# A routing table of 64-byte entries, three expert chunks loaded ahead of the rows, 17 chunk buffers and experts in program order

## The chip, the cores and the metric

The kernel runs on one core of a Trainium2 chip. The core has five engines that run their own instruction streams and wait for each other by semaphores: TensorE (PE; its weight loads are listed as PEld), VectorE (DVE), ScalarE (ACT), GpSimd (POOL) and SyncE (SP). Transfers are issued from the queues of SP, ACT and POOL and carried out by 16 DMA engines. The metric is the device time of one execution in microseconds; lower is better.

## The reference

Two transformer blocks follow each other on 512 tokens of 1024 features, all in float32. The first has sliding-window attention, a gated delta rule and an MLP; the second has retention and differential attention. All the edits lie in the mixture of experts that closes the second block:

```python
def hierarchical_moe(h, w_rg, b_rg, w_re, b_re, w1, w3, w2):
    gp = softmax(h @ w_rg + b_rg);  g_top, g_idx = top_k(gp, 1)        # 4 groups
    el = (h @ w_re + b_re).reshape(T, 4, 8) of the group g_idx
    e_val, e_idx = top_k(el, 2)                                        # 2 of 8 experts
    weights = g_top * softmax(e_val);  expert = g_idx * 8 + e_idx
    # each token goes through its two experts (of 32):
    y = sum over both of weights * ((silu(h @ w1[e]) * (h @ w3[e])) @ w2[e])
x = x + g2 * y
return rmsnorm(x, norm_final)
```

w1 and w3 are 1024 x 512 for each expert, w2 is 512 x 1024: 6 MB of weights per expert, 192 MB for all 32.

## The kernel before

After the projection `w_out` the kernel writes the block's rows to HBM (`x1_rows` stores x1d, `rows` stores the normalised h2d), routes the tokens (`route`, `tables`) and sorts the 1024 pairs of token and expert by expert. `weigh` stores a table `tab` (1024 entries of 8 bytes: token number and weight, in sorted order); `tables` makes the indices `ix` with which an expert's entries are found in it. `sorted_x` gathers the tokens' rows from h2d in sorted order, 128 at a time, with eight indirect DMAs on POOL's queue, transposes them on TensorE (tile pxs) and puts them into `xs`. Four of the eight rows lie in two chunk buffers (`spare`) that are lent for it.

Each expert is worked on in windows of the sorted pairs. The letters of `PLAN` say how many: H is half a window (64 pairs), F a full one (128), E one and a half, D two. The places in this list are filled at run time: an expert with more pairs comes to a larger place (`etab` holds which expert stands where, so chunk loads from place 3 on read their expert from `etab` into a register of SP). Places 0 to 2 are fixed.

The weights come in 1 MB chunks of 128 x 2048. An expert has six: 0 to 3 hold gate and up, 4 and 5 the down projection. They are loaded in one order, written out in `places`: four chunks of experts 0 and 1, their downs, and then for each expert j its chunks 0 and 1, the downs of j-1, and its chunks 2 and 3; last come the downs of expert 31. Before the change the chunks go in turn through 16 buffers: eight called eraw (pool r8, also used elsewhere) and eight spare. Chunks 0 to 7 are loaded during `w_out` (`ahead`); `fetch` issues six more after the last row store (`issue_after(self.rowed)`), two more behind the gathers, and `use` issues chunk n+16 where chunk n is used. The loads are issued on SP and wait there for their buffer.

In `experts`, `look` reads an expert's entries of `tab` by an indirect DMA on POOL's queue into a small tile `note` and doubles the token numbers for half windows on VectorE (L1929), since half windows write rows of 512. `up` computes gate and up into PSUM tiles ph (and pu), `gated` makes `es` from them (ACT and DVE), `turn` transposes it (paT, then ea on ACT), `down` multiplies with chunks 4 and 5 (py), scales by g2 on VectorE (ey) and scatters the result with an accumulating indirect DMA on POOL's queue, in turns to x1d and yd. Three notes are read ahead (`AHEAD`). A scheduler orders the instructions of each engine; in the expert loop TensorE's order too is the scheduler's choice.

The last two experts (`BIDE` = 30 and 31) aren't scattered: their results are added to the rows by one-hot matmuls (`closing`, `select`, `place`, tile pl). `gather` loads the rows of x1d and yd into tiles rowf (SP, L2048), POOL adds them (L2052), then come pl, the final norm and the store of `out`.

Of the kernel before, what the change touches and what calls it, by code (L numbers as in the profile page):

```python
# [9 lines left out]
F32 = mybir.dt.float32  # L10
# [7 lines left out]
P = 128  # L18
S = 512
# [7 lines left out]
NMORE = 8  # L27
# [24 lines left out]
PLAN = "HHHHHHHEHHHHHHHDHHHHHHHFHFHHHFHH"  # L52
# [227 lines left out]
class K:  # L280
# [1079 lines left out]
    def moe(self):  # L1360
        nc, tc, T = self.nc, self.tc, self.T
        with ExitStack() as es:
            mo = self.mo = es.enter_context(self.pool("mo"))
            with ExitStack() as sc:
                rp = sc.enter_context(self.pool("route", "right"))

                self.scraps = [[t, 0] for t in (self.cs, self.sn)]
                self.scraps += [[self.wp.tile([P, 1024], F32, name="scrap", tag=g, bufs=n), 0]
                                for g, n in (("wraw", 2), ("wraw", 2))]
                for g in ("c5", "c2"):  # L1370
                    self.ct[g] = self.scrap(rp, [_COFF[g][1]], g)
                    nc.sync.dma_start(self.ct[g], T[g])
                self.router_end(rp)
                self.x1_rows(0)
                self.rows()
                self.x1_rows(1)
                with ExitStack() as self.late:
                    self.tables(rp, self.route(rp))
            self.right.close()
            with ExitStack() as rs:  # L1380
                self.extra = rs.enter_context(self.pool("extra"))
                self.rowp = rs.enter_context(self.pool("rowp", "right"))
                self.post = rs.enter_context(self.pool("post", "right"))
                self.xs = self.post.tile([P, KT, 9 * P], F32, name="xs")
                self.g2 = self.post.tile([P, D], F32, name="g2row")
                self.g2h = self.post.tile([P, 512], F32, name="g2half")
                self.use, fetch = self.places()
                rows = [self.spare() for _ in range(2)]
                with self.tc.issue_after(self.rowed):
                    fetch(6 + NMORE)  # L1390
                self.sorted_x(rows)
                fetch(8 + NMORE)
                for b in range(2):
                    pg = self.pt("pg2")
                    self.rowbc(pg, self.mod[:, 5 * KT + 4 * b:5 * KT + 4 * b + 4], 4)
                    nc.scalar.activation(self.g2[:, b * 512:(b + 1) * 512], pg, AF.Copy)
                    h = slice(b * HALF, (b + 1) * HALF)
                    nc.vector.tensor_copy(self.g2h[h], self.g2[h, b * 512:(b + 1) * 512])
                self.experts()

    def eload(self, src):
        raw = self.wide("eraw") if self.nraw % (8 + NMORE) < 8 else self.spare()
        self.nraw += 1
        last = self.nc.sync.dma_start(raw, src)
        self.loaded = getattr(last, "ins", last)
        return raw

    def spare(self):
        return self.extra.tile([P, 2048], F32, name="spare", bufs=NMORE)

# [72 lines left out]
    def route(self, ap):  # L1483
# [90 lines left out]
        def weigh():  # L1574
# [34 lines left out]
            nc.scalar.dma_start(self.tab.rearrange("(b p) c -> p b c", p=P), sw)  # L1609
# [26 lines left out]
    def tables(self, ap, then):  # L1636
# [55 lines left out]
        V.scalar_tensor_tensor(off, off, BIG, wrow, op0=ALU.mult, op1=ALU.add)  # L1692
        self.ix = self.mo.tile([P, NBLK * NE], I32, name="ix")
        V.tensor_add(self.ix.rearrange("p (b e) -> p b e", b=NBLK), win, off)
# [25 lines left out]
    def note(self, ix):  # L1720

        nc = self.nc
        t = self.post.tile([P, 2], I32, name="note", bufs=NE + len(SECOND))
        nc.gpsimd.memset(t, int(BIG))
        nc.gpsimd.indirect_dma_start(
            out=t, out_offset=None, in_=self.tab[:, :], in_offset=bass.IndirectOffsetOnAxis(ap=ix, axis=0),
            bounds_check=2 * S - 1, oob_is_err=False)
        return t
# [21 lines left out]
    def sorted_x(self, more):  # L1750

        nc = self.nc
        nc.vector.memset(self.xs[:, :, 2 * S:], 0.0)
# [3 lines left out]
        for b, row in enumerate(rows):  # L1757
# [5 lines left out]
            for h in range(2):  # L1763
# [8 lines left out]
                else:  # L1772
                    nc.vector.tensor_add(dst, src, self.sh2[:, k].unsqueeze(2).to_broadcast([P, 4, P]))
        self.gathered = last.ins
# [34 lines left out]
    def gated(self, pss, ws):  # L1809
        nc = self.nc  # L1810
        out = []
        with self.tc.high_priority(offset=HP):
            for (few, g, u, _), w in zip(pss, ws):
                s = self.post.tile([P, 512], F32, name="es", bufs=3)
# [7 lines left out]
    def turn(self, few, s):  # L1822
# [6 lines left out]
        a = self.post.tile([P, 4, P], F32, name="ea", bufs=3)[:, :, :m]  # L1829
# [4 lines left out]
    def down(self, aa, use, ixs, stay=False):  # L1834
# [47 lines left out]
    def places(self):  # L1882
# [19 lines left out]
        def fetch(n):  # L1902
            nonlocal pos
            while pos < min(n, len(order)):
                self.raws[order[pos]] = self.eload(source(*order[pos]))
                pos += 1
# [6 lines left out]

    def experts(self):
        nc, tc, T = self.nc, self.tc, self.T
        ET = mybir.EngineType
        notes, self.tok, self.idx = {}, {}, {}
        windows = lambda j: [(b * NE + j, m) for b, m in enumerate(WIN[j])]

        def look(j):  # L1920

            notes[j] = [], []
            for i, m in windows(j):
                t = self.note(self.ix[:, i:i + 1])
                ix = t[:, 0:1]
                if m == HALF:

                    i2 = self.post.tile([P, 1], I32, name="note2", bufs=NE)
                    nc.vector.tensor_scalar(i2, ix, 2.0, self.c("side"), op0=ALU.mult, op1=ALU.add)  # L1929
                    if j >= BIDE:  # L1930
                        self.idx[j] = i2
                        self.tok[j] = self.mo.tile([P, 1], F32, name=f"tok{j}")
                        nc.vector.tensor_copy(self.tok[j], ix)
                    ix = i2
                notes[j][0].append(t[:, 1:2].bitcast(F32))
                notes[j][1].append(ix)

# [12 lines left out]
        with tc.issue_after(behind):  # L1950
            for j in range(AHEAD):
                look(j)
        for j in range(NE):
            if j == 0:
                xs = [self.xs[:, :, 0:HALF]]
            else:
                xs = [self.window(self.load(self.wtab[0:1, i:i + 1], 2 * S, ET.Activation), m) for i, m in windows(j)]
            pss = self.up_begin(xs)
            last = j - 1 if j - 1 in held else None
            for c in range(4):  # L1960
                if c == 2 and last is not None and j != 1:
                    turn(last)
                    down(last)
                    behind = self.scattered
                self.up(pss, c, self.use(j, c))
            held[j] = self.gated(pss, notes[j][0])
            if j == 1:
                for i in range(2):
                    turn(i)
                    down(i)  # L1970
                behind = self.scattered
            if j + AHEAD < NE:
                with tc.issue_after(behind):
                    look(j + AHEAD)
# [137 lines left out]
```

## Time and profile before

| what | value |
|---|---|
| runs | 1924.11 us median of 3 (1922.74 to 1925.02) |
| profiled execution | 1929.74 us |
| its span in the trace | 1927.9 us |
| PE busy | 1836.7 us (95%) |
| DVE, ACT, POOL busy | 833.5, 622.2, 305.7 us |
| bytes moved | 359.63 MB, mean 187 GB/s |
| granted TensorE clock, mean | 0.979 |

The span is what the trace covers; the execution's own time is 1.84 us longer. A row of a time line reads: start, duration, engine, line, operation, out<-in, count, and in brackets how long the engine was idle before and what ended that. The mean load of the DMA engines is low over the whole span, because the first three quarters are matmuls on weights that are loaded along the way; the expert stage fills the last quarter.

### The profile page before, as it was taken

Reading aid. Unit: us, or ns where it says so; the run is one execution under the profiler, and the core shown is the slowest. Engines: PE = TensorE matmul, PEld = TensorE weight load, DVE = VectorE, ACT = ScalarE, POOL = GpSimd, SP = SyncE. Lnnn points to the kernel's source line nnn. Section 1 sums busy time; section 2 is a strip of 40 time slices with the busy share of each in tenths; the row PEclk is TensorE's granted clock in tenths of the full one; section 3 lists DMA queues with packets and bytes.
Section 4 is the critical chain, followed back from the end, with each engine's and each line's share of the span. In section 5 each row is a group of like instructions: output and inputs, shape, how many; then the busy total and the mean of one; then the engine's idle time right before and its main releaser. Section 6 shows DMA issues by size and latency. Waiting matters only on the chain.

```text
span 1927.9 us, 23285 instructions
## 1 busy us (share of the span) xinstructions
PE 1836.7 (95%) x8926; PEld 1315.3 (68%) x8926; DVE 833.5 (43%) x1561; ACT 622.2 (32%) x1031; POOL 305.7 (16%) x290
## 2 busy tenths in 40 slices
PE   8999999999999999999999999999879987999984
PEld 6888898788888888888777888888633322333322
DVE  6666656565565666654424343443411110110114
ACT  6454534433232344644442333322321110111102
POOL 0122122100000002421110000002212121121113
PEclk9999999899999999999999999999889999999998
DMA  5321004344554532222222222344779999999995
GB/s 184 88 66 39 6 23 142 90 156 164 186 186 159 194 114 91 80 71 73 77 60 89 92 82 80 120 164 169 271 282 404 417 402 414 381 395 417 404 419 209
DMA packets 76290, 359.63 MB, mean 187 GB/s; under 512 B 13034, under 2 KB 13546, under 8 KB 48528
## 3 DMA queue, kind: packets, MB, share of 16 engines
q1 hardware_dynamic: 63104, 321.55, 44.7%
q0 software_dynamic: 10304, 33.60, 5.6%
q10 hardware_dynamic: 2768, 2.96, 0.5%
q8 instruction: 71, 1.16, 0.2%
q14 instruction: 43, 0.35, 0.1%
HBM read 345.48 MB, written 18.36 MB: 189 GB/s over the span
## 4 chain that ended last, share of the span: by engine, by line
PE 82%; DMA 13%; DVE 2%; issue 1%; ACT 1%; POOL 0%; SPq 0%; POOLq 0%; ACTq 0%; DVEq 0%
PE acc L345 16%; PE acc L346 16%; PE acc L347 16%; DMA spare<-in_w_exp 7%; PE ph L1785 5%; DMA eraw<-in_w_exp 4%; PE py L1785 3%; PE py L1849 2%; PE po L1200 2%; PE acc L1172 2%; PE acc L1174 2%; PE acc L1173 2%; PE pu L1807 1%; DMA tab<-sw 1%; PE ph L1807 1%; PE pu L731 1%
## 5 line engine op out<-in xcount | busy, mean ns | idle before, releaser
L345 PE MATMUL acc<-u,whi 128*128 128x512 f32 x920 | 367.0, 400 | 2.2 <-ACT mg L1191 2.0
L346 PE MATMUL acc<-u,whi 128*128 128x512 f32 x920 | 364.7, 397 | 2.4 <-DVE u L322 2.3
L317 ACT ACTIVATE whi<-wraw 128x1024 fp32r<-128x1024 f32 x193 | 204.3, 1059 | 499.5 <-PE acc L346 401.5
L347 PE MATMUL acc<-u,wlo 128*128 128x512 f32 x920 | 362.3, 394 | 0.4 <-DVE wlo L318 0.4
L318 DVE TENSOR_TENSOR wlo<-wraw,whi 128x1024 fp32r<-128x1024 f32 x193 | 239.5, 1241 | 193.9 <-ACT whi L317 187.5
L346 PEld LDWEIGHTS acc<-u,whi 128*128 128x128 f32 x920 | 174.3, 189 | 40.2 <-DVE u L322 3.9
L345 PEld LDWEIGHTS acc<-u,whi 128*128 128x128 f32 x920 | 174.0, 189 | 39.3 <-ACT mg L1191 2.4
L347 PEld LDWEIGHTS acc<-u,wlo 128*128 128x128 f32 x920 | 174.0, 189 | 38.0 <-DVE wlo L318 1.0
L1785 PE MATMUL ph<-eraw,ex 128*64 128x512 f32 x480 | 115.1, 603 | 10.7 <-DMA eraw<-in_w_exp 10.4
L1818 DVE SCALAR_TENSOR_TENSOR es<-es,note,ph 64x512 f32<-64x512 f32 x28 | 21.1, 754 | 196.3 <-ACT es L1817 196.2
L1785 PE MATMUL ph<-spare,ex 128*64 128x512 f32 x384 | 94.2, 619 | 11.8 <-DMA spare<-in_w_exp 11.6
L1817 ACT ACTIVATE es<-ph 64x512 f32<-64x512 f32 (+1 forms) x34 | 20.1, 590 | 263.2 <-PE ph L1785 200.1
L345 PE MATMUL acc<-ah,whi 128*128 128x512 f32 x256 | 99.4, 389 | 0.0
L346 PE MATMUL acc<-al,whi 128*128 128x512 f32 x256 | 99.0, 389 | 0.0
L347 PE MATMUL acc<-ah,wlo 128*128 128x512 f32 x256 | 98.9, 389 | 0.0
L1785 PEld LDWEIGHTS ph<-eraw,ex 128*64 128x64 f32 x480 | 34.3, 138 | 75.7 <-issue 59.3
L1785 PEld LDWEIGHTS ph<-spare,ex 128*64 128x64 f32 x384 | 26.8, 141 | 71.0 <-issue 49.6
L1172 PE MATMUL acc<-whi,u 128*128 128x256 f32 x256 | 73.1, 286 | 0.0
L1173 PE MATMUL acc<-whi,u 128*128 128x256 f32 x256 | 72.6, 284 | 0.0
L1174 PE MATMUL acc<-wlo,u 128*128 128x256 f32 x256 | 72.5, 284 | 0.0
L1785 PE MATMUL py<-spare,ea 128*64 128x512 f32 x272 | 62.5, 595 | 3.2 <-ACT ea L1831 3.2
L1855 DVE TENSOR_TENSOR ey<-py,g2half 128x512 f32<-128x512 f32 x28 | 19.2, 690 | 105.0 <-PE py L1785 102.3
(549 smaller groups left out, 3005.4 us busy)
## 6 DMA issues: line engine op xcount, KB each, us to landing
eraw<-in_w_exp SPq DMA_DIRECT2D x96, 1024.0 KB, 19.9
spare<-in_w_exp SPq DMA_DIRECT2D x96, 1024.0 KB, 20.5
wraw<-in_w_in SPq DMA_DIRECT2D x87, 512.0 KB, 3.6
adaw<-in_w_ada POOLq DMA_DIRECT2D x24, 1024.0 KB, 5.1
wraw<-in_w_up SPq DMA_DIRECT2D x32, 512.0 KB, 3.6
wraw<-in_w_down SPq DMA_DIRECT2D x32, 512.0 KB, 5.5
hT<-in_xT SPq DMA_DIRECT2D x16, 256.0 KB, 5.5
wraw<-in_w_o SPq DMA_DIRECT2D x8, 512.0 KB, 3.6
```

Source lines behind the costliest of these rows:

```text
L317: a = nc.scalar.activation(hi, src, AF.Copy)
L318: b = nc.vector.tensor_sub(lo, src, hi.bitcast(F32))
L345: nc.tensor.matmul(ps, hi[:, ws], uh[k], start=(start and k == 0), stop=False)
L346: nc.tensor.matmul(ps, hi[:, ws], ul[k], start=False, stop=False)
L347: nc.tensor.matmul(ps, lo[:, ws], uh[k], start=False, stop=(stop and k == n - 1))
L1172: nc.tensor.matmul(o, uh[k][:, tok], hi[:, m], start=(k == 0), stop=False)
L1173: nc.tensor.matmul(o, ul[k][:, tok], hi[:, m], start=False, stop=False)
L1174: nc.tensor.matmul(o, uh[k][:, tok], lo[:, m], start=False, stop=(k == KT - 1))
L1200: nc.tensor.matmul(po[:, kt * P:], v[:, kt, e * P:(e + 1) * P], w[:, kt, kt * P:], start=(kt == 0), stop=(kt == NT - 1))
L1785: self.nc.tensor.matmul(ps[i * HALF:(i + 1) * HALF], lhs, rhs[i], start=start, stop=stop)
L1807: self.nc.tensor.matmul(ps, x[:, k, :], y, **st)
L1849: nc.tensor.matmul(p, a[:, k, :], y, **st)
```

## The change

1. `tab` is stored with one descriptor per partition (`(p b) c`): each partition's eight entries, 64 bytes, lie together. The indices `ix` are turned to that layout with a shift and an and (three more operations on VectorE).
2. A pool `early` with three buffers `sooner` is opened at the start of `moe`. Chunks 8 to 10 are issued on SP there, ahead of the stores of x1d and h2d.
3. The ring has 17 buffers: eight eraw, three sooner, six spare.
4. Chunks 11 to 14 are issued on POOL's queue behind the third note; 15 and 16 on SP behind the gathers.
5. `xs`'s padding is set to zero and the tokens are doubled behind the last addition of the shift (`self.added`). All notes lie in one tile `lists`, the doubled ones in `twice`.
6. A half window's ey is made by two multiplications of 64 rows from g2 (the tile g2half is gone). es and ea have two buffers, not three.
7. TensorE works in program order in the loop over the experts (`with self.in_order()`).
8. `PLAN` has the same letters, in part at other places: E 7 to 6, D 15 to 13, F 23, 25, 29 to 19, 22, 25.

```diff
-NMORE = 8
+NMORE = 9
+EARLY = 3
-PLAN = "HHHHHHHEHHHHHHHDHHHHHHHFHFHHHFHH"
+PLAN = "HHHHHHEHHHHHHDHHHHHFHHFHHFHHHHHH"
@@ moe
+            self.early = es.enter_context(self.pool("early"))
+            self.use, fetch = self.places()
+            fetch(8 + EARLY)
...
-                self.use, fetch = self.places()
-                rows = [self.spare() for _ in range(2)]
-                with self.tc.issue_after(self.rowed):
-                    fetch(6 + NMORE)
-                self.sorted_x(rows)
+                self.sorted_x([self.spare() for _ in range(2)])
+                self.begin()
+                with self.tc.issue_after(self.noted):
+                    fetch(6 + NMORE, nc.gpsimd)
                 fetch(8 + NMORE)
@@ eload
+        i = self.nraw % (8 + NMORE)
+        raw = self.wide("eraw") if i < 8 else self.sooner() if i < 8 + EARLY else self.spare()
+        last = (queue or self.nc.sync).dma_start(raw, src)
@@ weigh
-            nc.scalar.dma_start(self.tab.rearrange("(b p) c -> p b c", p=P), sw)
+            nc.scalar.dma_start(self.tab.rearrange("(p b) c -> p b c", p=P), sw)
@@ tables
+        V.tensor_add(ra, win, wrow)
+        V.tensor_scalar(rb, ra, 7, None, op0=ALU.logical_shift_right)
+        V.tensor_scalar(ra, ra, 127, 3, op0=ALU.bitwise_and, op1=ALU.logical_shift_left)
+        V.scalar_tensor_tensor(off, off, BIG, ra, op0=ALU.mult, op1=ALU.add)
+        V.tensor_add(self.ix.rearrange("p (b e) -> p b e", b=NBLK), off, rb)
@@ sorted_x
+        self.gathered, self.added = last.ins, add.ins
+        with self.tc.issue_after(add.ins):
+            nc.vector.memset(self.xs[:, :, 2 * S:], 0.0)
@@ down
-                    nc.vector.tensor_mul(y, ps[0], self.g2h)
+                    for b in range(2):
+                        h = slice(b * HALF, (b + 1) * HALF)
+                        nc.vector.tensor_mul(y[h], ps[0][h], self.g2[h, b * 512:(b + 1) * 512])
@@ look
+                with self.tc.issue_after(self.added):
+                    nc.vector.tensor_scalar(i2, ix, 2.0, self.c("side"), op0=ALU.mult, op1=ALU.add)
@@ begin
+        with self.tc.issue_after(self.gathered):
+            for j in range(AHEAD):
+                self.look(j)
@@ experts
+        with self.in_order():
+            for j in range(NE):
```

On POOL's queue, at the gathers of the rows (into spare and row), the program before reads all four first notes at once and goes on to the first scatters:

```order
L1759 DMA spare<-h2d,slot 128x1024 x4
L1759 DMA row<-h2d,slot 128x1024 x4
L1724 MEMSET note 128x2 x4
L1725 DMA note<-tab,ix 128x2 x4
L1870 DMA yd<-ey,note_10873 1024x512
L1870 DMA x1d<-ey,note_10880 1024x512
```

At the same place of the changed program the notes are called lists, and chunks of weights (spare<-in_w_exp) stand between the third and the fourth:

```order
L1768 DMA spare<-h2d,slot 128x1024 x4
L1768 DMA row<-h2d,slot 128x1024 x4
L1734 MEMSET lists 128x2 x4
L1735 DMA lists<-tab,ix 128x2 x3
L1406 DMA spare<-in_w_exp 128x2048 x4
L1735 DMA lists<-tab,ix 128x2
L1883 DMA yd<-ey,twice 1024x512
```

Four chunk loads have moved to this queue, behind the gathers and three notes.

On SP, from the last load of w_out to the first loads of the ring, the program before stores the rows first:

```order
L327 DMA wraw<-in_w_out 128x1024 x3
L1372 DMA scrap<-in_c 128x513
L1634 DMA x1d<-x1row 128x512 x4
L1624 DMA h2d<-h2row 128x1024 x4
L1634 DMA x1d<-x1row 128x512 x4
L1404 DMA spare<-in_w_exp 128x2048 x6
L2005 TENSOR_LOAD xtab
```

The changed program has there, with three chunks ahead of the stores:

```order
L329 DMA wraw<-in_w_out 128x1024 x3
L1377 DMA scrap<-in_c 128x513
L1406 DMA sooner<-in_w_exp 128x2048 x3
L1639 DMA x1d<-x1row 128x512 x4
L1629 DMA h2d<-h2row 128x1024 x4
L1639 DMA x1d<-x1row 128x512 x4
L2032 TENSOR_LOAD xtab
```

The six loads behind the stores are gone from SP; three stand ahead of them.

On TensorE, the end of the expert loop (ph are ups, py downs, paT the transposes, pl the closing matmuls) reads before, from expert 30's chunks 2 and 3 on:

```order
L1785 MATMUL ph<-eraw,ex 64x512 x8
L1785 MATMUL ph<-spare,ex 64x512 x8
L1828 MATMUL paT<-ct_c_93,es 128x128 x4
L1849 MATMUL py<-eraw,ea 128x512 x8
L1785 MATMUL ph<-spare,ex 64x512 x8
L1828 MATMUL paT<-ct_c_93,es 128x64 x4
L1785 MATMUL py<-spare,ea 64x512 x8
L1828 MATMUL paT<-ct_c_93,es 128x64 x4
L1785 MATMUL py<-spare,ea 64x512 x8
L1748 MATMUL pl<-closing 128x512 x32
```

and in the changed program, from expert 29's transposes on:

```order
L1839 MATMUL paT<-ct_c_93,es 128x64 x4
L1796 MATMUL py<-sooner,ea 64x512 x4
L1796 MATMUL py<-spare,ea 64x512 x4
L1796 MATMUL ph<-spare,ex 64x512 x16
L1839 MATMUL paT<-ct_c_93,es 128x64 x4
L1796 MATMUL py<-spare,ea 64x512 x4
L1796 MATMUL py<-eraw,ea 64x512 x4
L1796 MATMUL ph<-eraw,ex 64x512 x8
L1758 MATMUL pl<-closing 128x512 x4
```

Before, the full down of expert 29 (py 128x512) stands behind the first ups of expert 31; now the down of 29 is a half one and stands before them, and the ups and downs follow in the order of the loads.

## Rows read from the trace of the kernel before

**Rows 1.** Page, part 2: GB/s in 40 equal slices of the span.
```profile
GB/s 184 88 66 39 6 23 142 90 156 164 186 186 159 194 114 91 80 71 73 77 60 89 92 82 80 120 164 169 271 282 404 417 402 414 381 395 417 404 419 209
```
**Rows 2.** Stretches: length, busy us of each engine, PEclk, DMA share, GB/s.
```profile
1380.00:1405.00 25.00, 19.31 (x85) 11.62 (x86) 6.34 (x28) 4.45 (x16) 5.39 (x10) 0.66 1.02 418
...
1420.00:1430.00 10.00, 8.50 (x49) 7.22 (x50) 5.04 (x9) 6.32 (x19) 0.00 (x0) 0.70 0.14 60
...
1675.00:1700.00 25.00, 25.00 (x101) 9.47 (x101) 4.21 (x6) 1.99 (x4) 7.09 (x7) 1.00 0.90 308
1700.00:1880.00 180.00, 167.63 (x642) 59.89 (x638) 21.29 (x41) 21.70 (x37) 32.02 (x34) 0.99 1.02 414
...
1886.00:1888.00 2.00, 2.00 (x7) 0.53 (x7) 1.55 (x4) 0.00 (x0) 0.00 (x0) 1.00 0.89 369
1888.00:1890.00 2.00, 2.00 (x12) 0.72 (x10) 0.00 (x0) 0.00 (x0) 1.55 (x1) 1.00 0.54 221
```
**Rows 3.** Time line of SP's queue: start, us until the last was issued.
```profile
1366.38 3.79 SPq L1624 DMA_DIRECT2D h2d<-h2row  x4
...
1706.96 18.14 SPq L1404 DMA_DIRECT2D eraw<-in_w_exp  x8
...
1854.20 18.05 SPq L1404 DMA_DIRECT2D spare<-in_w_exp  x8
```
**Rows 4.** Time line of POOL and DVE, from the rows' places to the first note.
```profile
1376.31 1.15 POOL L1759 DMA_INDIRECT spare<-h2d,slot  x1 [21.77 <-DVE cs L1577]
...
1385.12 0.18 DVE L1608 TENSOR_REDUCE sw<-pwts 128x8 f32<-128x24 f32 x1 [4.17 <-PE keep L397]
...
1385.72 0.99 POOL L1759 DMA_INDIRECT row<-h2d,slot  x1 [0.30 <-issue]
...
1387.96 0.19 DVE L1683 COPY scrap<-porder 128x32 f32<-128x32 f32 x1 [2.44 <-PE pxs L401]
...
1389.94 0.29 DVE L1694 TENSOR_TENSOR ix<-scrap 128x160 int32<-128x160 f32 x1
...
1409.83 1.01 POOL L1725 DMA_INDIRECT note<-tab,ix  x1 [19.29 <-DMA tab<-sw]
```
**Rows 5.** Chain of work that ended last: start, us, what.
```profile
1385.33 23.73 DMA tab<-sw
...
1413.75 6.66 DMA note<-tab,ix
...
1428.45 7.09 PE ph L1785 x32
...
1668.86 13.93 PE py L1849 x32
...
1880.03 6.29 PE py L1849 x14
1888.17 8.68 DMA x1d<-ey,note
1896.86 3.20 DMA rowf<-x1d
```
**Rows 6.** Time line of POOL at the end.
```profile
1900.37 9.80 POOL L2052 TENSOR_TENSOR rowf<-rowf 128x1024 f32<-128x1024 f32 x4 [10.65 <-PE py L1785]
```
**Rows 7.** Page, DMA issues: count, KB each, median us to landing.
```profile
adaw<-in_w_ada POOLq DMA_DIRECT2D x24, 1024.0 KB, 5.1
```
**Rows 8.** Groups by shape, 1432 to 1880: busy us, mean ns, idle before.
```profile
L1855 DVE TENSOR_TENSOR ey<-py,g2half 128x512 f32<-128x512 f32 x26 | 17.9, 690 | 99.1 <-PE py L1785 96.5 <-DMA x1d<-ey,note 2.4
```
**Rows 9.** Stretches with TensorE's waits for chunks, columns as in rows 2.
```profile
1575.00:1580.00 5.00, 1.85 (x10) 0.40 (x6) 0.00 (x0) 0.00 (x0) 2.52 (x3) 0.96 1.02 416
1580.00:1585.00 5.00, 2.73 (x8) 0.88 (x10) 0.00 (x0) 0.00 (x0) 0.00 (x0) 0.50 1.02 408
...
1610.00:1615.00 5.00, 2.18 (x10) 0.68 (x12) 0.00 (x0) 0.00 (x0) 2.85 (x5) 1.00 1.02 412
```

More of the change, by code (lines that the diff above doesn't have):

```diff
@@ L1396, in moe, with eload @@
                     nc.scalar.activation(self.g2[:, b * 512:(b + 1) * 512], pg, AF.Copy)
-                    h = slice(b * HALF, (b + 1) * HALF)
-                    nc.vector.tensor_copy(self.g2h[h], self.g2[h, b * 512:(b + 1) * 512])
                 self.experts()
-    def eload(self, src):
-        raw = self.wide("eraw") if self.nraw % (8 + NMORE) < 8 else self.spare()
+    def eload(self, src, queue=None):
+        i = self.nraw % (8 + NMORE)
+        raw = self.wide("eraw") if i < 8 else self.sooner() if i < 8 + EARLY else self.spare()
         self.nraw += 1
-        last = self.nc.sync.dma_start(raw, src)
+        last = (queue or self.nc.sync).dma_start(raw, src)
         self.loaded = getattr(last, "ins", last)
@@ L1752, in sorted_x @@
         nc = self.nc
-        nc.vector.memset(self.xs[:, :, 2 * S:], 0.0)
         rows = [x[:, i * D:(i + 1) * D] for x in more for i in range(2)]
@@ L1900, in places, with fetch @@
         assert list(self.raws) == order[:pos]
-        def fetch(n):
+        def fetch(n, queue=None):
             nonlocal pos
             while pos < min(n, len(order)):
-                self.raws[order[pos]] = self.eload(source(*order[pos]))
+                self.raws[order[pos]] = self.eload(source(*order[pos]), queue)
                 pos += 1
@@ L1912, in places, with windows, look, begin @@
         return use, fetch
+    def windows(self, j):
+        return [(b * NE + j, m) for b, m in enumerate(WIN[j])]
+    def look(self, j):
+        nc = self.nc
+        self.notes[j] = [], []
+        for i, m in self.windows(j):
+            n = self.seen
+            self.seen += 1
+            t = self.note(self.ix[:, i:i + 1], self.lists[:, n])
+            ix = t[:, 0:1]
+            if m == HALF:
+                i2 = self.twice[:, n:n + 1]
+                with self.tc.issue_after(self.added):
+                    nc.vector.tensor_scalar(i2, ix, 2.0, self.c("side"), op0=ALU.mult, op1=ALU.add)
+                if j >= BIDE:
+                    self.idx[j] = i2
+                    self.tok[j] = self.mo.tile([P, 1], F32, name=f"tok{j}")
+                    nc.vector.tensor_copy(self.tok[j], ix)
+                ix = i2
+            self.notes[j][0].append(t[:, 1:2].bitcast(F32))
+            self.notes[j][1].append(ix)
+    def begin(self):
+        n = sum(len(w) for w in WIN)
+        self.notes, self.tok, self.idx, self.seen = {}, {}, {}, 0
+        self.lists = self.post.tile([P, n, 2], I32, name="lists")
+        self.twice = self.post.tile([P, n], I32, name="twice")
+        with self.tc.issue_after(self.gathered):
+            for j in range(AHEAD):
+                self.look(j)
     def experts(self):
@@ L1916, in experts @@
         ET = mybir.EngineType
[L1917 to L1936, printed above, removed]
+        notes, look = self.notes, self.look
+        windows = self.windows
         held = {}
@@ L1949, in experts @@
         behind = self.gathered
[L1950 to L1963, printed above, removed]
-                    behind = self.scattered
[L1965 to L1974, printed above, removed]
+        with self.in_order():
+            for j in range(NE):
+                if j == 0:
+                    xs = [self.xs[:, :, 0:HALF]]
+                else:
+                    xs = [self.window(self.load(self.wtab[0:1, i:i + 1], 2 * S, ET.Activation), m) for i, m in windows(j)]
+                pss = self.up_begin(xs)
+                last = j - 1 if j - 1 in held else None
+                for c in range(4):
+                    if c == 2 and last is not None and j != 1:
+                        turn(last)
+                        down(last)
+                        behind = self.scattered
+                    self.up(pss, c, self.use(j, c))
+                held[j] = self.gated(pss, notes[j][0])
+                if j == 1:
+                    for i in range(2):
+                        turn(i)
+                        down(i)
+                    behind = self.scattered
+                if j + AHEAD < NE:
+                    with tc.issue_after(behind):
+                        look(j + AHEAD)
         self.closing()
```

23 lines of the change are left out of this document (11 added, 12 removed).

## The prediction, made before the changed kernel ran

> **What bounds the kernel now.** I first read the page's GB/s by slices: from about slice 31 on the core moves 400 GB/s or more [rows 1]. This is the expert stage, where 192 chunks of 1 MB are loaded, and there TensorE waits for transfers. The table of stretches shows the stream at 412 to 418 GB/s in 1380:1405 and 1700:1880, and three places where it isn't: 60 GB/s in 1420:1430, 308 in 1675:1700, and its end, where the rate falls from 369 to 221 GB/s around 1888 [rows 2]. The queue of SP gives the price of one chunk: batches of eight start at 1706.96 and, seven batches later, at 1854.20 [rows 3], so (1854.20 - 1706.96) / 56 = 2.63 us. What decides the span is therefore when the stream starts to run without a gap, the price of a chunk, and what follows the last chunk.
>
> The start, from the timeline: the rows' places are there at 1376.3, when the first of eight gathers is issued on POOL, and the last is issued at 1385.72; the table's second column is reduced at 1385.12 and the indices ix are made at 1389.94; but the first note is read at 1409.83 [rows 4]. The chain of waits says why: the store of the table `tab` took 23.73 us, then the fourth note 6.66 us, and expert 1's first matmuls run at 1428.45 [rows 5]. Only they free a further buffer: 16 buffers plus the four chunks of expert 0 make 20 chunks, all landed by then, hence the gap of 1420:1430. The stream resumes at about 1432 and has 172 chunks left: 172 x 2.63 = 452, plus 25 x (1 - 308/414) = 6.4 us for the dip of 1675:1700, gives 1890, against the 1888 to 1889 that the table shows. I use 2.62 and 1888.
>
> The dip lies beside the 13.93 us down of the expert with two full windows, at 1668.86, which stands there later than its chunks' turn [rows 5]. At the end the full expert 29's down starts at 1880.03, its scatter is issued at 1888.17 and lands 8.68 us later; only then, at 1896.86, are the rows of x1d loaded [rows 5], and POOL's four adds start at 1900.37, 12.4 us after the stream's end. They take 9.80 us [rows 6], to 1910.2, and 17.7 us follow to the span's end at 1927.9.
>
> **The change, part by part.**
>
> *Table of 64-byte entries.* One descriptor per partition, 128 packets in place of 1024. Before, the store took 23.73 us beside a stream that was running at 418 GB/s [rows 2, 5]. No row shows the new form, so from both sides: as slow as before, 23.7 us, or as a small store with little ahead of it, for which the nearest row is the note's read, 6.66 us [rows 5]; linear in packets it would be 23.73 / 8 = 3.0 us. I take 5: the packets are fewer, and by the other parts no weights are queued ahead of it. It lands at 1385.3 + 5 = 1390.3. The Trainium skill ("DMA: Bandwidth & Descriptors", section "Queues, rings and completion order") says that each DMA engine goes round between the queue rows packet by packet, so each small packet waits behind a packet of weights; the 23.73 us agree with it, and by it the new store would be near the 3 us. The same page's table of specifications asks for 512 bytes per transfer for full rate, which 64 bytes are not; no row here shows what that costs.
>
> *Three more operations for ix.* Before, ix came at 1389.94 + 0.29 [rows 4]; three operations like it make 1391.1. In front of them VectorE stood still 4.17 us ahead of the table's second column and 2.44 us ahead of the copy of `porder`, both after TensorE [rows 4]. If these stalls go with the traffic, ix is there at 1384.5; if not, 1391.1.
>
> *Three chunks ahead.* Chunks 8 to 10 stand on SP before the rows' stores. They move 3 MB, about 8 us, where the row stores run (four h2d stores from 1366.38 [rows 3]). The gathers start at 1376.31; if h2d lands late they slip, by 0 to 3 us. I take 0.
>
> *Chunks 11 to 14 behind three notes, on POOL.* The gathers now have the DMA engines to themselves. The last is issued at 1385.72 + 0.99 [rows 4], so the notes start at the later of 1387, tab and ix: between 1387 and 1391. Three notes at 1.3 us (the distance of the gathers) end at 1391 to 1395. The loads then take about 5.1 us to land, as the loads of w_ada on POOL's queue do [rows 7], of which 2.6 are the transfer: the stream starts at T = 1393.5 to 1397.5, and I take 1395.5, with 11 chunks landed. Chunks 15 and 16 go on SP beside them. From there on expert 0's and 1's matmuls (their rows are there by about 1400) free buffers faster than 2.62 us each: a half expert's chunk is 8 of the 32 matmuls of 7.09 us [rows 5], 1.77 us. Against before, at 1432 with 20 landed, this is 1432 - 1395.5 - 9 x 2.62 = 12.9 us. It would be worth nothing at T = 1408.4.
>
> *17th buffer.* With T = 1395.5 no chunk waits for a buffer in my sum, with 16 or 17: 0 us.
>
> *Program order on TensorE.* Down and up run in the order of the loads. The late down no longer holds eight buffers: the 6.4 us dip should go. Costs: a half expert is 48 matmuls, 10.6 us, and about 1 us for its turn, beside 6 x 2.62 = 15.7 us of loads; nothing.
>
> *Doubling, memset, half ey in two.* One more VectorE operation of 0.69 us for each half expert [rows 8], beside 15.7 us; its two matmul-side buffers (es, ea) fall from 3 to 2, and in load order only one expert is held. If the cover went it would be 27 x 0.69 = 19 us spread out; I put 0.
>
> *The list.* The same letters, but the last full expert is 25, not 29. Expert 29's half down stands ten chunks before the stream's end, so its scatter (8.68 us) lands ahead of it. The loads of rows then follow the last chunk directly in the queue: eight of 0.5 MB, 1.31 us each; the third gives the first pair, at 3.9 us after the stream's end, and the last pair 10.5 us after. The adds run from about 4 to 13.7 us after the end (2.36 each, the last waits for its load), where before they ran from 12.4 to 22.2: 8.5 us.
>
> **The sum.** Stream's end: 1395.5 + 181 x 2.62 = 1869.7. Adds' end 1883.4, and 17.7 us more: span 1901.1, that is 26.8 us less than 1927.9. The profiled execution was 1929.74, 1.84 over its span and 5.6 over the median of the runs, 1924.11. So 1901.1 + 1.84 - 5.63 = 1897.3; I say 1898.
>
> **Rivals.**
>
> *Late start (1907).* The stalls of VectorE stay and the notes or POOL's loads are late, T about 1405: 9.5 us lost. For it: POOL now has loads, notes and gathers in one line. Against: nothing in that line waits for weights.
>
> *The table stays slow (1918).* If 64-byte entries still take 23.7 us, notes start at 1409 and T = 1415.4, which is 7 us worse than before's start; the dip's 6.4 and the tail's 8.5 us stay: about 8 us faster in all, 1916 to 1918. Against: nothing is queued with it.
>
> *Tail not gained (1906).* The rows' buffers are those of the last chunks in the ring of 17 (the end of TensorE's rows shows py and ph from `eraw`), so loads of rows could wait for the last matmuls. By the order of the waits they are free before the end; if not, 8.5 us.
>
> *Faster stream (1886).* In 1700:1880 the whole core moves 414 GB/s [rows 2], 2.53 us a chunk if all were weights; at 2.56, 181 x 0.06 = 11 us more.
>
> *Slower than before: TensorE's clock.* With program order TensorE waits at each chunk. In 1580:1585 its granted clock was 0.50, the lower of its two levels (1.2 of 2.4 GHz), after it had been busy 1.85 us of the 5 before; in 1610:1615 it was 1.00 with 2.18 us busy in 5 [rows 9]. At the lower level a half expert takes 21.2 + 1 = 22.2 us, more than 15.7: TensorE would be the bound, 6.5 us lost for each such expert. Five experts eat the 27 us; from there on it is slower than 1928 (1930 and more). Against: with 1.77 us of matmuls a chunk and waits of 0.85 us it would be busier than in 1610:1615, and a TensorE that is late is busy all the time, with which the clock was 1.00 in 1700:1880 (0.99) [rows 2]. The Trainium skill ("TensorE: Matmul & The Clock Gate", section "HAM oscillation — how this bites in real kernels") describes just this, waits for transfers between short groups of matmuls that keep the clock low; by that it would be this rival, and the trace bears it out only for the long waits.
>
> **Chances and range.** Forecast 0.60, late start 0.13, faster stream 0.10, tail not gained 0.08, slow table 0.04, lower clock 0.03, nothing moved 0.02. The bounds of the forecast's own terms are T 1393.5 to 1397.5, a chunk at 2.58 to 2.65 (7 us less, 5 more), gathers up to 3 us later: 1889 to 1906. Taking in the faster stream and the late start: 1886 to 1909. About 0.2% (4 us) is what a measurement of this kernel can tell from no change. Faster 0.94, same 0.02, slower 0.04.
>
> **What would show it.** The tab store should last 3 to 7 us; the first note be issued at 1387 to 1391; 400 GB/s or more from 1397 to 1870 without the gap of 1420:1430 and without a dip where the two-window expert is; TensorE's matmuls waiting under 1 us for each chunk at a clock of 1.00; x1d's rows loaded within a few us of the last chunk. I am wrong if the loads on POOL's queue come late, if buffers and not transfers set the pace with program order, or if the clock falls.

## The result and the profile after

The changed kernel takes 1905.45 us (median of 4 runs, 1903.03 to 1906.06) against 1923.88 us before; the ratio is 0.9894, 95% interval 0.9877 to 0.9912. It is faster by 18.4 us, inside the range and short of the 26 us forecast. Its profiled execution took 1906.06 us, with a span of 1904.3.

The page's GB/s by slices of the span, and the granted clock in tenths:

```profile
PEclk9999999999999999999999999999989999999997
GB/s 186 88 68 40 7 23 134 104 156 164 188 186 157 182 128 100 70 78 77 67 62 88 95 83 70 133 149 218 192 373 404 410 407 418 399 409 412 411 415 201
```

The 30th slice moves 373 GB/s in place of 282 in [rows 1]; the clock stayed at its upper level through the expert stage.

The two profiled executions differ by 6.1 us ahead of the first gather. Of the change only the three early loads move into that stretch, and without them (u_early below) the gather comes at 1369.99 us, against 1370.23 with them; so I take the 6.1 us for scatter between executions and count from that gather. POOL's time line of the changed kernel has the first gather, the first note and the loads on POOL's queue; SP's has the last chunks and the loads of rows:

```profile
1370.23 1.14 POOL L1768 DMA_INDIRECT spare<-h2d,slot  x1 [21.77 <-DVE cs L1582]
...
1386.69 1.01 POOL L1735 DMA_INDIRECT lists<-tab,ix  x1 [2.76 <-DVE xs L1782]
...
1390.31 2.20 POOL L1406 DMA_DIRECT2D spare<-in_w_exp  x4
```

```profile
1842.22 10.52 SPq L1406 DMA_DIRECT2D eraw<-in_w_exp  x5
1854.85 2.76 SPq L2075 DMA_DIRECT2D rowf<-yd  x2
1866.28 0.80 SPq L2075 DMA_DIRECT2D rowf<-x1d  x2
```

The chain of waits of the changed kernel, at expert 1's first matmuls and behind the last chunk:

```profile
1405.50 7.11 PE ph L1796 x32
...
1858.40 7.83 DMA x1d<-ey,twice
1866.28 9.98 DMA rowf<-x1d
1876.52 1.05 POOL rowf L2079
```

| us after the first gather | before | changed |
|---|---|---|
| first note issued | 33.5 | 16.5 |
| expert 1's first matmuls | 52.1 | 35.3 |
| last chunk issued | 495.9 | 482.5 |
| POOL's first add of rows | 524.1 | 506.3 |
| end of the span | 551.6 | 534.1 |

(Before: [rows 3 to 6]; 495.9 is 1854.20 + 18.05 - 1376.31, 482.5 is 1842.22 + 10.52 - 1370.23.) Of 17.5 us, 13.4 are there when the last chunk is issued, and 4.4 more come between that and the first add; the rest took 0.3 us longer.

### The profile page after: what moved, and what is told of

Same layout as the page of the kernel before. It is cut to its first block, busy times and chain, and to the rows that moved or that the text cites. A ratio compares the mean times of both kernels' runs of the same rounds, so it can differ in the third digit from the quotient of the medians.

```text
span 1904.3 us, 23342 instructions
## 1 busy us (share of the span) xinstructions
PE 1824.3 (96%) x8926; PEld 1304.4 (69%) x8926; DVE 850.6 (45%) x1590; ACT 622.1 (33%) x1031; POOL 309.0 (16%) x294
## 4 chain that ended last, share of the span: by engine, by line
PE 67%; DMA 11%; DVE 2%; ACT 1%; issue 1%; POOL 0%; ACTq 0%; SPq 0%; POOLq 0%; DVEq 0%
PE acc L347 13%; PE acc L349 13%; PE acc L348 13%; PE ph L1796 7%; DMA eraw<-in_w_exp 5%; PE py L1796 3%; DMA sooner<-in_w_exp 3%; DMA spare<-in_w_exp 2%; PE po L1202 2%; PE acc L1174 2%; PE acc L1176 2%; PE acc L1175 2%; PE ph L1818 1%; PE py L1860 1%; PE pu L1818 1%; PE pds L1243 1%
## 5 line engine op out<-in xcount | busy, mean ns | idle before, releaser
L1829 DVE SCALAR_TENSOR_TENSOR es<-es,lists,ph 64x512 f32<-64x512 f32 x28 | 21.1, 754 | 219.6 <-ACT es L1828 219.6
L1796 PE MATMUL ph<-eraw,ex 128*64 128x512 f32 x480 | 109.6, 597 | 6.0 <-DMA eraw<-in_w_exp 5.0
L1868 DVE TENSOR_TENSOR ey<-py,g2row 64x512 f32<-64x512 f32 x56 | 38.6, 688 | 67.1 <-PE py L1796 66.2
L1188 POOL TENSOR_TENSOR rot<-rot,sn 128x512 f32<-128x512 f32 x24 | 33.6, 1400 | 195.5 <-ACT rot L1186 108.5
L1796 PE MATMUL ph<-spare,ex 128*64 128x512 f32 x264 | 59.9, 595 | 5.3 <-DMA spare<-in_w_exp 5.3
L942 POOL DMA_DIRECT2D adaw<-in_w_ada x24 | 13.0, 542 | 301.1 <-DVE modT L946 301.1
```

Source lines behind the costliest of these rows:

```text
L1796: self.nc.tensor.matmul(ps[i * HALF:(i + 1) * HALF], lhs, rhs[i], start=start, stop=stop)
L1868: nc.vector.tensor_mul(y[h], ps[0][h], self.g2[h, b * 512:(b + 1) * 512])
```

## The experiments

All start from the changed kernel, and a label that begins with u undoes the parts that it names. Medians are in us; "from" is the range of the runs. The kernel before measured 1923.46 to 1925.28 beside them.

| run | undone or altered | median (from, to) |
|---|---|---|
| changed | - | 1905.45 (1903.03, 1906.06) |
| u_tab | 1, table's layout | 1906.25 (1904.88, 1906.62) |
| u_pool | 4, loads on POOL's queue | 1898.91 (1897.47, 1901.13) |
| u_tabpool | 1 and 4 | 1903.76 (1901.80, 1904.56) |
| u_tabpooldouble | 1, 4 and the doubling of 5 | 1911.96 (1908.62, 1914.97) |
| u_early | 2, early loads | 1912.54 (1909.98, 1914.42) |
| u_ring16 | 16 buffers | 1903.00 (1902.66, 1903.94) |
| u_order | 7, program order | 1907.07 (1904.41, 1908.71) |
| u_plan | 8, list | 1902.98 (1902.16, 1906.22) |
| u_planorder | 7 and 8 | 1909.32 (1905.08, 1911.35) |
| u_four | 1, 4, 7 and 8 | 1916.73 (1913.72, 1921.86) |
| pool16 | 4 undone, 16 buffers | 1902.20 (1899.57, 1902.31) |
| no_scat | 26 of 32 scatters left out | 1901.13 (1899.15, 1903.59) |

**The start: table and queue.** u_tab:

```diff
-            nc.scalar.dma_start(self.tab.rearrange("(p b) c -> p b c", p=P), sw)
+            nc.scalar.dma_start(self.tab.rearrange("(b p) c -> p b c", p=P), sw)
...
```

The part left out here gives `ix` the form that it had before.

> The changed kernel with part 1 alone undone: tab again in 8-byte entries (1024 packets), ix as before it. Theory A (the store took 23.73 us because its packets waited behind packets of weights; in the changed kernel no weights are queued at that time): the store lands within about 8 us of its issue, the notes start at most 3 us later, time 1904 to 1909 us. Rival B (the number of packets alone makes the 23.73 us): the notes start about 17 us later than in the changed kernel and the time is 1914 to 1922 us.

u_pool:

```diff
-                self.sorted_x([self.spare() for _ in range(2)])
+                rows = [self.spare() for _ in range(2)]
+                with self.tc.issue_after(self.rowed):
+                    fetch(6 + NMORE)
+                self.sorted_x(rows)
                 self.begin()
-                with self.tc.issue_after(self.noted):
-                    fetch(6 + NMORE, nc.gpsimd)
```

> The changed kernel with part 4 alone undone: chunks 11 to 14 are issued on SP right behind the row stores, so that gathers and table run beside weights; the 64-byte entries stay. Theory A: 8 packets per DMA engine wait behind weights in place of 64, so the store takes 3 to 6 us, the gathers 14 us or more to land; DMA engines idle less ahead of the notes, time within 5 us of the changed kernel's 1905. Rival C (it is the free queue during the gathers that gives the gain): the gathers and so expert 0's first matmuls come late and the time is 1910 to 1920 us.

u_tabpool has both edits.

> Parts 1 and 4 both undone (8-byte entries, chunks 11 to 14 on SP behind the row stores), the rest as changed. Theory A: the store again takes 15 us or more beside the weights, the notes and expert 1 come late, a gap in the stream returns; time 1913 to 1922 us, most of the gain gone. Rival (list, program order and 17 buffers make the gain): 1905 to 1909 us.

The table's store and the first note that waits for it, from the time line of u_tab (8-byte entries, no weights queued when it is issued, the gathers of rows beside them):

```profile
1375.90 0.39 ACTq L1614 DMA_DIRECT2D tab<-sw  x1
1386.82 1.01 POOL L1732 DMA_INDIRECT lists<-tab,ix  x1 [6.98 <-DMA tab<-sw]
```

the chain of u_tabpool (8-byte entries beside weights):

```profile
1376.57 19.09 DMA tab<-sw
```

its time line at the first note:

```profile
1396.43 1.01 POOL L1733 DMA_INDIRECT lists<-tab,ix  x1 [16.38 <-DMA tab<-sw]
```

the store in the changed kernel (its first note, at 1386.69, is shown above):

```profile
1380.68 0.34 ACTq L1614 DMA_DIRECT2D tab<-sw  x1
```

and the time line of u_pool (64-byte entries beside weights):

```profile
1379.50 0.34 ACTq L1615 DMA_DIRECT2D tab<-sw  x1
1386.07 1.01 POOL L1736 DMA_INDIRECT lists<-tab,ix  x1 [3.21 <-DMA tab<-sw]
```

From the store's issue to the first note it is 10.9 us with small entries and few weights, 19.9 with small entries beside weights, 6.6 with 64-byte entries beside weights, and at most 6.0 in the changed kernel, where the note waited for VectorE and not for the table. In u_tab three quarters of the store's packets were through by 1381.1, 5.2 us after its issue, and only the rest ran beside a chunk, whose first packet starts at 1383.4. So the long store had both causes: taking most of the weights away saves 9.0 us, larger entries save 13.3, and both together some 14. But u_tab costs 0.8 us, within the runs' scatter; u_tabpool, at 1903.76, is under both of its expected ranges and 1.7 us faster than the changed kernel, with ranges that overlap; and u_pool is faster by 6.5 us, more than the 5 us that I had allowed: the loads' new place is a loss. The stretches of the two kernels show why; the changed kernel:

```profile
1370.00:1375.00 5.00, 4.00 (x35) 3.75 (x33) 4.45 (x43) 1.80 (x4) 3.85 (x4) 1.00 0.58 172
1375.00:1380.00 5.00, 2.78 (x22) 2.53 (x22) 0.00 (x0) 0.00 (x0) 3.78 (x5) 1.00 0.93 322
1380.00:1385.00 5.00, 1.77 (x8) 1.14 (x8) 3.47 (x19) 0.00 (x0) 0.85 (x5) 0.65 0.94 354
1385.00:1390.00 5.00, 3.34 (x8) 1.12 (x10) 1.95 (x7) 2.17 (x8) 2.70 (x3) 0.50 0.47 141
1390.00:1395.00 5.00, 5.00 (x21) 1.84 (x18) 0.00 (x0) 0.00 (x0) 3.58 (x6) 0.83 0.87 304
```

and u_pool:

```profile
1375.00:1380.00 5.00, 4.02 (x22) 3.65 (x22) 2.01 (x19) 0.00 (x0) 4.01 (x4) 0.74 0.95 391
...
1385.00:1390.00 5.00, 5.00 (x16) 2.38 (x17) 0.69 (x1) 1.48 (x6) 3.02 (x4) 0.50 1.04 426
...
1395.00:1400.00 5.00, 5.00 (x32) 2.87 (x31) 1.99 (x4) 2.86 (x10) 0.00 (x0) 1.00 0.83 291
```

The last but one column is the DMA engines' busy share. In the changed kernel they idle 5 x (0.42 + 0.07 + 0.06 + 0.53 + 0.13) = 6.1 us while the loads wait behind the notes, in u_pool about 1.1 us (the two stretches left out have shares of 1.01). Part of these 5 us belongs to this one execution, because VectorE stood still for longer ahead of the table's second column ("remote" means that the profile does not name what ended the wait); the changed kernel:

```profile
1380.47 0.18 DVE L1613 TENSOR_REDUCE sw<-pwts 128x8 f32<-128x24 f32 x1 [5.58 <-remote]
```

and u_pool:

```profile
1379.28 0.18 DVE L1614 TENSOR_REDUCE sw<-pwts 128x8 f32<-128x24 f32 x1 [2.67 <-remote]
```

In u_ring16 (below), with the loads behind the notes and 2.69 us of standing still, the same five stretches idle 3.3 us. A trace also keeps the time and size of each DMA packet, and the chunks are its packets of 8 KB, 128 to a chunk. 60 us after the first gather 27.0 chunks had landed in the changed kernel and 29.5 in u_pool; 2.5 chunks at 2.66 us (the price found below) are 6.7 us, and u_pool's last such packet ends 495.2 us after the gather against 501.9, 6.7 us earlier. It agrees with theory M (below): the amount is fixed, so idle time ahead of the last chunk is paid. How much the loads' place costs depends on the rest: 6.5 us here, 2.5 with 8-byte entries (u_tab against u_tabpool), and 0.8, within the scatter, with 16 buffers (u_ring16 against pool16, below).

**The start: early loads and buffers.** u_early:

```diff
-EARLY = 3
+EARLY = 0
```

> The changed kernel without the early loads: chunks 8 to 14 all come on POOL's queue behind the third note, 17 buffers stay. Theory M (the stream's end is its amount over its pace, so each microsecond in which the DMA engines idle ahead of it costs one): 3 chunks move out of a stretch that is otherwise empty, 3 x 2.65 = 8 us, time 1911 to 1915 us. Rival N (the first matmuls of experts 0 and 1 set the start, and the loads have slack): 1904 to 1907 us.

It costs 7.1 us; theory M holds, with 3 x 2.66 = 8.0 us as its price. By the packets 24.9 chunks had landed at 60 us, 2.1 fewer than in the changed kernel, and the last packet ends 4.8 us later, at 506.7. u_ring16:

```diff
-NMORE = 9
+NMORE = 8
```

> The changed kernel with 16 buffers (five spare in place of six). The forecast's term of 0 us for the 17th buffer: 1904 to 1907 us. Rival (a chunk less is in flight while the DMA engines wait for experts 0 and 1, or SP waits for matmuls in the stream): 2.6 us or more, 1908 to 1912 us.

The 17th buffer brings nothing here (2.5 us less time without it, with ranges that overlap, and 1 us under the expected range). pool16 has that edit and u_pool's.

> Chunks 11 to 13 on SP right behind the row stores (as in the run of 1898.91 us, with one chunk less) and 16 buffers, everything else as changed. If the 17th buffer is worth nothing: 1896 to 1901 us. If it is worth a chunk once the queue starts early: 1901 to 1904 us.

With the loads on SP, 16 buffers are 3.3 us slower than 17; the ranges overlap, so a worth of about one chunk there is likely, not certain.

**The start: the doubling.** u_tabpooldouble is u_tabpool with one edit more:

```diff
-                with self.tc.issue_after(self.added):
+                with ExitStack():
                     nc.vector.tensor_scalar(i2, ix, 2.0, self.c("side"), op0=ALU.mult, op1=ALU.add)
```

> Parts 1 and 4 undone, as in the run that measured 1903.76, and besides the doubling of the tokens no longer held behind the shift, so that the first doublings stand between the shift's additions on VectorE, as before the change. If the late notes hurt before the change because the additions, and with them expert 1, stood behind the doublings: expert 1's matmuls come 5 to 10 us later than with the doubling behind, a gap in the stream, 1909 to 1915 us. Rival (the additions behind expert 0's gate wait for the same note anyway): 1903 to 1906 us.

VectorE's time line in u_tabpooldouble, where the additions (xs) stand behind the doublings:

```profile
1404.92 0.21 DVE L1941 TENSOR_SCALAR twice<-lists,ct_c 128x1 int32<-128x1 int32 x1 [10.70 <-DMA lists<-tab,ix]
...
1409.06 1.28 DVE L1780 TENSOR_TENSOR xs<-pxs,modT 128x512 f32<-128x512 f32 x2
```

and in u_tabpool, where only expert 0's gate (es) stands between them:

```profile
1402.50 0.75 DVE L1827 SCALAR_TENSOR_TENSOR es<-es,lists,ph 64x512 f32<-64x512 f32 x1 [8.27 <-DMA lists<-tab,ix]
1403.28 1.88 DVE L1780 TENSOR_TENSOR xs<-pxs,modT 128x512 f32<-128x512 f32 x3
```

Expert 1's matmuls start 45.8 us after the first gather against 39.1, and the time is 8.2 us longer. So with a late table the place of the doubling, which I had put at 0, is worth as much as the early loads.

**The end: order and list.** u_order replaces `with self.in_order():` by `with ExitStack():`.

> The changed kernel without program order on TensorE in the loop over the experts. Forecast's step (the late down of the two-window expert costs a dip of 5 to 6 us in the stream): 1909 to 1913 us, a dip in GB/s near that expert. Rival D (the pace of the stream is that of the slowest DMA engine, 2.67 us per chunk, and the dip in the mean rate costs nothing): 1903 to 1907 us even if a dip shows.

u_plan has the old list:

```diff
-PLAN = "HHHHHHEHHHHHHDHHHHHFHHFHHFHHHHHH"
+PLAN = "HHHHHHHEHHHHHHHDHHHHHHHFHFHHHFHH"
```

> The changed kernel with the old list (full experts 23, 25 and 29). Theory L (the list shortens what follows the last chunk: full expert 29's scatter lands late and the rows of x1d wait for it): POOL's first add 26 to 29 us after the last chunk's issue in place of 23.8, the stream's end as in the changed kernel, time 1908 to 1911 us. Rival (program order alone brings 29's down early enough): first add at 24 us, 1904 to 1907 us.

u_planorder has both edits, u_four those of u_tabpool besides.

> The changed kernel with the old list and without program order, as before the change in both. The part of the gain that the start doesn't give should be here: first add 28 us after the last chunk's issue, the last issue as in the changed kernel (482 us after the first gather), time 1909 to 1912 us. Rival (order and list also set the stream's pace): last issue later by 3 us or more, 1913 to 1917 us.

> Parts 1, 4, 7 and 8 undone together: 8-byte entries, chunks 11 to 14 on SP behind the row stores, the scheduler's order on TensorE, the old list. What stays is the three early loads, 17 buffers and the doubling behind the shift (with the small edits of part 6). If the parts add up: 1903.76 (parts 1 and 4 undone) + 3.87 (parts 7 and 8: 1909.32 - 1905.45) = 1907.6 us, so about 16 us of the gain come without the table's layout, POOL's queue, the order and the list. Rival (the table's late landing needs program order or the list to be harmless): 1911 to 1918 us.

Without program order the dip is there again, in two stretches of u_order:

```profile
1600.00:1610.00 10.00, 10.00 (x40) 3.57 (x40) 3.08 (x5) 1.27 (x2) 0.72 (x1) 1.00 0.86 343
1610.00:1620.00 10.00, 10.00 (x45) 3.82 (x42) 0.97 (x2) 2.31 (x4) 2.04 (x3) 1.00 1.02 416
1620.00:1630.00 10.00, 10.00 (x25) 4.48 (x24) 0.44 (x1) 0.00 (x0) 0.00 (x0) 1.00 0.69 263
```

By the mean rate that is 1.7 + 3.6 = 5.3 us lost. The changed kernel has a shallow dip at the same place, behind the downs of its expert with two windows:

```profile
1620.00:1630.00 10.00, 9.47 (x47) 3.31 (x48) 1.44 (x2) 1.61 (x3) 3.74 (x4) 1.00 1.03 361
1630.00:1640.00 10.00, 9.47 (x48) 3.15 (x46) 2.26 (x4) 1.60 (x3) 2.54 (x3) 1.00 1.02 396
```

It is 1.3 + 0.4 = 1.7 us by the mean rate, with the DMA engines busy throughout. In u_order the last chunk is nevertheless issued 482.7 us after the first gather, as in the changed kernel (482.5), and the time is 1.6 us longer, within the scatter. The time lies between the two expectations' ranges, at rival D's edge. In this execution expert 1 started 3.4 us earlier (31.9 us after the gather), which may hide part of a loss. By the packets 28.2 chunks had landed at 60 us, a lead of 1.2 chunks or 3.2 us over the changed kernel, and the last packet ends at 502.2 us against 501.9, so about 3.5 us were lost on the way; in u_four, without program order too, 27.0 chunks at 60 us end at 502.2, and nothing was lost. The dip costs less than its 5.3 us, and whether it costs nothing stays open.

From the last chunk's issue to the span's end it is 51.6 us in the changed kernel, 53.0 in u_order, 53.5 in u_plan, 60.1 in u_planorder and 60.0 in u_four, against 51.4 in u_tabpool. Order and list stand in for each other: one of them alone keeps most of the end short, without both it is 8.5 us longer. The first add follows the issue after 23.8 us in u_order, 25.9 in u_plan and 31.7 in u_planorder. Theory L had more than that for u_plan, whose time, 1902.98 us, is no longer than the changed kernel's and under both expected ranges. In the profiles of u_plan and u_planorder VectorE did not stand still ahead of the table, so expert 1 starts at 26.2 us and the last issue is at 475 us, 7 us early; the medians, not these starts, are compared. By them u_planorder is 3.9 us slower than the changed kernel (ranges overlap a little), as expected, and u_four 13.0 us slower than u_tabpool. My expectation for u_four, which added up 1907.6, missed: the rival held. What u_four keeps over the kernel before is 8.6 us (1916.73 against 1925.28 beside it), for the early loads, the 17th buffer, the place of the doubling and part 6 together.

**The pace of the stream.** no_scat:

```diff
+        if self.nscat <= 4 or self.nscat > 30:
             self.scattered = self.nc.gpsimd.indirect_dma_start(
...
```

> The changed kernel with 26 of the 31 accumulating scatters left out (the output lacks those experts' results). Theory S (the last chunk waits for the slowest of 16 DMA engines, which falls behind the others by what the scatters and other small transfers give it): the mean rate no longer falls off over 8 us ahead of the last chunk, a chunk costs 2.55 us, time 1880 to 1890 us. Rival (the scatters cost their bytes only, about 4 MB at 410 GB/s): 1894 to 1898 us, and the fall-off stays.

The end of the stream in stretches, changed kernel:

```profile
1858.00:1860.00 2.00, 1.63 (x10) 0.47 (x6) 1.43 (x6) 0.28 (x1) 1.55 (x1) 1.00 0.99 381
1860.00:1862.00 2.00, 1.84 (x8) 0.48 (x8) 0.00 (x0) 0.11 (x1) 0.00 (x0) 1.00 0.88 359
1862.00:1864.00 2.00, 1.85 (x10) 0.48 (x8) 0.00 (x0) 0.00 (x0) 0.00 (x0) 1.00 0.72 285
1864.00:1866.00 2.00, 1.24 (x8) 0.48 (x8) 1.38 (x2) 0.35 (x1) 0.00 (x0) 1.00 0.57 230
1866.00:1868.00 2.00, 1.46 (x10) 0.29 (x6) 0.69 (x1) 0.28 (x1) 0.00 (x0) 1.00 0.63 199
```

and TensorE's time line in them:

```profile
1864.94 1.94 PE L1796 MATMUL ph<-eraw,ex 128*64 128x512 f32 x8 [0.76 <-DMA eraw<-in_w_exp]
...
1867.42 1.94 PE L1796 MATMUL ph<-eraw,ex 128*64 128x512 f32 x8 [0.54 <-DMA eraw<-in_w_exp]
```

TensorE waits for chunks at 1864.9 and 1867.4, while the DMA engines together are busy 0.57 and 0.63 of the time: most of the 16 are through with the stream, some are not, and a chunk has landed only when the last part has. The packets show it too: of the chunks' packets 16 are under way at 1856, 12 at 1860, 7 at 1864, 4 at 1866 and 1 at 1870, and the last twelve run one behind the other, 0.31 us each, from 1868.3 to 1872.1, as they would on a single engine, whose share of a chunk is 8 packets. The last 2.9 chunks took 16.1 us, while in the middle a chunk took 2.61 us (1400 to 1620) and 2.59 us (1640 to 1856). In no_scat the rate stays up to 1864 and only one stretch falls:

```profile
1862.00:1864.00 2.00, 2.00 (x12) 0.69 (x10) 0.00 (x0) 0.00 (x0) 0.00 (x0) 1.00 1.01 412
1864.00:1866.00 2.00, 2.00 (x12) 0.72 (x10) 0.00 (x0) 0.00 (x0) 0.00 (x0) 1.00 0.82 299
1866.00:1868.00 2.00, 2.00 (x11) 0.43 (x6) 0.00 (x0) 0.00 (x0) 0.00 (x0) 1.00 0.96 371
```

The uneven end goes with the scatters, as theory S said (5.7 chunks landed in the last 16.1 us), but its time missed, and the rival's too: 4.3 us gained. This run does not give the price of the scatters, because its edit did more than leave them out. The notes of later experts wait for scatters, so POOL read all that were left in one row, from 1452.15 to 1486.57; around its end TensorE stood still for 13.21 us, behind a wait of ACT that the profile does not explain:

```profile
1489.75 5.65 PE L1796 MATMUL py<-eraw,ea 128*64 128x512 f32 x16 [13.21 <-ACT ea L1842]
```

and then the DMA engines idled in mid-stream:

```profile
1500.00:1510.00 10.00, 10.00 (x37) 3.02 (x36) 2.20 (x7) 2.46 (x4) 0.00 (x0) 1.00 0.84 319
1510.00:1520.00 10.00, 9.70 (x34) 3.37 (x32) 0.00 (x0) 0.87 (x2) 0.00 (x0) 1.00 0.79 288
1520.00:1530.00 10.00, 10.00 (x44) 3.17 (x40) 5.03 (x16) 1.22 (x2) 0.00 (x0) 1.00 0.70 247
1620.00:1630.00 10.00, 9.75 (x30) 4.67 (x29) 0.00 (x0) 1.09 (x2) 0.00 (x0) 1.00 0.85 344
1630.00:1640.00 10.00, 10.00 (x36) 3.76 (x36) 2.87 (x5) 0.70 (x2) 0.00 (x0) 1.00 0.61 211
```

These five stretches idle 10 x (0.16 + 0.21 + 0.30 + 0.15 + 0.39) = 12.1 us. From 1650 to 1860 a chunk took 2.50 us, under theory S's 2.55. What the scatters cost without that idle time stays open.

## Why the prediction was right, point by point

The direction, the range and the two places of the gain were right; the gain in the sum was 8 to 9 us too large, and the credit for the start went to the wrong edits. That the time still lies inside the range is in part luck: 1905.45 us is at the upper edge of the forecast's own bounds (1889 to 1906), the price of a chunk, 2.66 us, is outside its bounds (2.58 to 2.65), and only u_pool, which lacks part 4, comes near the 1898 us that I named.

- **Start of the stream.** Forecast: T = 1395.5, which is 19.2 us after the first gather, with the loads on POOL's queue issued 14.7 to 18.7 us and the first note 11 to 15 us after it. Measured: the rate comes up at 1391, 20.8 us after the gather, the loads are issued at 20.1 and the first note at 16.5. T is right but for 2 us. VectorE's stall ahead of the table's second column stayed; it was 5.58 us in this execution, 2.70 in u_tab's and none in u_plan's, so one profile gives the start only to some 5 us.
- **Table store, 5 us.** At most 6.0. Right. That it is needed for the gain was wrong: u_tabpool, with a store of 19.09 us, is as fast as the changed kernel.
- **Loads behind the notes.** I had reckoned T from them and not asked what the DMA engines do until then. That idle time is the cost: 6.5 us, against u_pool.
- **Early loads, doubling.** The first was inside the sum as 11 chunks landed (worth 7.1 us measured); the second I put at 0. It is 8.2 us where the table is late, and unmeasured where it is early.
- **The dip of 6.4 us that should go, and the chunk at 2.62 us.** This is the step that failed. The last packet of a chunk ends at 1872.1; from 1391, where the rate comes up, 181 chunks took 481.1 us, 2.66 each. Before, with the last packet at 1891.4, it was (1891.4 - 1432) / 172 = 2.67 with the dip inside. The deep dip went, a shallow one stayed, and the price of a chunk over the whole stream did not fall. 181 x 0.04 = 7.2 us, and with the 2 us of the start this is the missing 9 us. In the middle the price was as forecast (2.61 and 2.59); the excess is at the end, where 2.9 chunks took 16.1 us, 8.5 more than at 2.62. The sum had no term for it.
- **End of the stream at 1888 before.** I took the fall of the mean rate for the last landing, which came at 1891.4. Counted from there, the first add came 9.0 us later before, and 4.4 us later in the changed kernel, where I had forecast 4: the tail's own step was right, and its gain is 4.5 us, not 8.5, because the start of the count was wrong.
- **Rows' buffers.** They were free in time: the rows of x1d were issued when the scatter had landed (1866.28), and waited in the queue behind the last chunk.
- **Clock.** 1.00 in every stretch of 10 us from 1400 to 1870; the slower rival did not come.

That the end of the stream waits for the last of the DMA engines is shown by the packets of the changed kernel, and no_scat's even end ties it to the scatters or to the notes that wait for them. A packet's record does not name its engine, so why one falls behind stays open; that the dip before the change was free because that engine stayed busy in it is argued, not shown.

## What to carry to other kernels

When a fixed amount must be streamed, count the microseconds in which the DMA engines idle ahead of its last transfer: moving loads out of the way of a small urgent transfer (here 6.5 us, less in other combinations) costs more than it brings if that transfer can be made robust instead, by fewer packets or by taking what waits for it out of other work's line on its engine. Undo edits singly and in pairs: here the list and the order, and the layout and the queue, stood in for each other, the 17th buffer seemed to help only with the loads on SP, and none of these pairs adds up. And take a stream's price from the landing of its last transfer: in its middle a chunk cost 2.6 us, over the whole stream 2.66. The best version found keeps every edit but the loads on POOL's queue: 1898.91 us, ratio to before 0.9866 (0.9850 to 0.9882).

## What the runs showed of the hardware

The store of 1024 entries of 8 bytes took 10.9 us to its reader where only its last quarter met weights, and 19.9 beside weights; as 128 entries of 64 bytes it took 6.6 us even beside weights. The mean DMA rate is no measure of when a transfer lands: at the end of the stream it falls over 8 us while chunks are still awaited, and the last twelve packets of 8 KB run one at a time, for 3.8 us.
